# The query stage of a product-key expert layer in one pass or in two passes by tokens

## Chip, core and metric

The kernel runs on one core of one Trainium2 chip. The metric is the device time of one execution in microseconds (us); lower is better. TensorE does the matmuls, VectorE, ScalarE and POOL (GpSimd) the elementwise work, and SP issues most DMAs.

## What is computed

One step of a hybrid encoder layer for 512 prompt tokens and 128 sample tokens (640 in all, five tiles of 128). A recurrent group and a window attention feed `h = x + W_out [...]`; then a product-key expert layer is added, and this is the part that the change touches:

```python
def peer(xn, w_query, sub_keys1, sub_keys2, expert_u, expert_v):
    q = (xn @ w_query).reshape(T, PEER_HEADS, 2, D_HALF)          # 8 heads, two halves of 128
    s1 = jnp.einsum('thd,kd->thk', q[:, :, 0], sub_keys1)          # 128 keys each
    s2 = jnp.einsum('thd,kd->thk', q[:, :, 1], sub_keys2)
    v1, i1 = lax.top_k(s1, PEER_TOPK)                              # 16 best of each half
    v2, i2 = lax.top_k(s2, PEER_TOPK)
    cand_s = (v1[..., :, None] + v2[..., None, :]).reshape(T, PEER_HEADS, 256)
    ...
    top_s, top_pos = lax.top_k(cand_s, PEER_TOPK)
    idx = jnp.take_along_axis(cand_i, top_pos, axis=-1)            # of 16384 experts
    gates = jax.nn.softmax(top_s, axis=-1)
    u = expert_u[idx]
    act = jax.nn.gelu(jnp.einsum('thkd,td->thk', u, xn))
    return jnp.einsum('thk,thkd->td', gates * act, expert_v[idx])
```

## The kernel before

**Two ways to the experts.** The first 448 tokens (`SD`) go the dense way: all 16384 experts are multiplied with them, in `NS` = 64 pairs of 256 experts, first with the u slabs (lines 1285 to 1333), then with the v slabs (1339 to 1365); the gates stand as a matrix with zeros in DRAM (`Gd`). The last 64 prompt tokens and the 128 sample tokens are the "own" tokens (tiles 3 and 4): their expert rows are gathered by indirect DMAs on POOL's queue (`fetch`, line 1167), and VectorE multiplies or adds each row (`consume`, 1177). There are `NO` = 384 such rows of 128 x 1024, six buffers for them (`RING`), and `own_work` deals them out over the pairs once tile 4 is selected.

**Split operands.** Every slab of weights (128 x 2048, 1 MB) comes by an SP DMA into `raw` (`load_slab`, 88). ScalarE copies it into `wh` (`high`, 93), and VectorE or POOL subtracts to get the remainder `wl` (`low`, 98). Each of the three has two buffers. A product takes three matmuls for each of the eight blocks of the contraction: `wh` with `xh`, `wh` with `xl`, `wl` with `xh`. `next_slab` (222) prepares the next slab of the list `order` (213) and then issues the load of a later one.

**Query stage.** Each of the eight slabs of `w_query` holds 256 query columns of one head, hence two units of 128 columns: `u` from 0 to 15. Units 0 and 1 are computed in halves (`query_half`, 853) between the transposes of the five token tiles (`turn_rows`, 830), and the others in the loop from 939: `proj_T` (106) with 48 matmuls of 320 columns, then `query_keys(u - 2)` (907) with five score tiles, each an fp32 matmul that takes two instructions, two copies of the scores on ScalarE, and the search for the 16 best of each tile on VectorE; then, in every second unit, `next_slab(G)` with its subtraction on POOL; then the copy of the queries out of PSUM (`query_out`, 903). The schedule is manual: each engine runs its instructions in the order written.

**Plan of the pairs.** What is left of the selection is cut into pieces with estimated costs (`piece`, 988): for each tile `select` (candidates, `best` twice four times, `exponents` with an act on ScalarE, two `index`, `gates`), and for the dense tiles `matrix` (56 pieces `hot`, each with matmuls and copies). Lines 1201 to 1219 deal them out: tiles 4 and 3 first with at most 6.6 per pair, and the others evenly up to pair 58. In pair `c` VectorE runs the subtraction for slab `c + 1` (POOL does so for `c` up to 2), then `own_work(c)`, then the pieces of the pair.

Of the kernel before, what the change touches and what calls it, by code (L numbers as in the profile page):

```python
# [7 lines left out]
F32 = mybir.dt.float32  # L8
# [8 lines left out]
P = 128  # L17
# [4 lines left out]
T = S + NB * TS  # L22
# [26 lines left out]
def hybrid_layer(ctx: ExitStack, tc: tile.TileContext, i, o):  # L49
# [16 lines left out]
    def wide():  # L66
        return pss.tile([P, 2, 512], F32, name="pa", tag="pa", bufs=2)
# [35 lines left out]
    def kc(w, c=256):  # L103
        return [x.rearrange("p (k c) -> p k c", c=c) for x in w]
# [89 lines left out]
    for k in range(KD):  # L194
# [16 lines left out]


    order = [i["w_qkv"][0], i["w_u"][0], i["w_u"][1], i["w_qkv"][1], i["w_gate"][0], i["w_gate"][1]] \
        + [i["w_out"][n] for n in range(4)] + [i["w_query"][n] for n in range(PH)]
    slab_raw, slabs = [], []

    def fetch_slab():
# [604 lines left out]
    def mean_square(t):  # L822
        xn[t] = wk.tile([P, D], F32, name="xn", tag=("p", "pT")[t % 2], bufs=2)
        A.activation(xn[t], h_rows[:, t], AF.Square, accum_out=ssq[:, t:t + 1])
        rsqrt(rh, rv_h, ssq[:, t:t + 1], slice(t, t + 1), D)

    def scaled(t):
        V.scalar_tensor_tensor(xn[t], h_rows[:, t], rh[:, t:t + 1], g2b, op0=ALU.mult, op1=ALU.mult)

    def turn_rows(t, halves=(0, 1)):  # L830

        ts_ = slice(t * P, (t + 1) * P)
        for hf in halves:
            pt = bank().rearrange("p (k c) -> p k c", k=4)
            for k in range(4):
                PE.transpose(pt[:, k], xn[t][:, (4 * hf + k) * P:(4 * hf + k + 1) * P], ident)
            A.activation(xh[:, 4 * hf:4 * hf + 4, ts_], pt, AF.Copy)
            V.tensor_sub(xl[:, 4 * hf:4 * hf + 4, ts_], pt, xh[:, 4 * hf:4 * hf + 4, ts_].bitcast(F32))

    for t in range(NT):  # L840
        merge_attn(0, t)
    next_slab(V)
    for t in range(ND):
        merge_attn(1, t)
        nc.sync.dma_start(Hd[t], h_rows[:, t])
        if t:
            scaled(t - 1)
        mean_square(t)
    merge_attn(1, 4)
    xh, xl = parts_tile()  # L850
    two = [wide(), wide()]

    def query_half(n, hf):
        wh, wl = kc(slabs[A0 + 2])
# [5 lines left out]
    for hf in range(2):  # L860
        for t in range(3):
            turn_rows(t, (hf,))
    scaled(3)
    query_half(0, 0)
    mean_square(4)
    turn_rows(3)
    nc.sync.dma_start(X3, xn[3][HD:])
    scaled(4)
    nc.sync.dma_start(Xd, xn[ND])
    query_half(1, 0)  # L870
    turn_rows(4)
    for n in range(2):
        query_half(n, 1)
    close_wk()


# [23 lines left out]
    tq, close_tq = open_pool("tq")  # L900
    qt = {}

    def query_out(u, ps):
        q = qt[u] = tq.tile([P, T], F32, name="q", tag="q", bufs=2)
        A.activation(q.rearrange("p (a b) -> p a b", a=2), ps[:, :, :H2], AF.Copy)

    def query_keys(u):
        c, n = u // 2, u % 2
        s = tq.tile([P, NT, NK], F32, name="s", tag="s", bufs=2)
        q = qt.pop(u)  # L910
        for t0, t1 in ((0, 4), (4, 5)):
            sc = bank()[:, :(t1 - t0) * P]
            for t in range(t0, t1):
                PE.matmul(sc[:, (t - t0) * P:(t - t0 + 1) * P], q[:, t * P:(t + 1) * P], sk[n],  # L914
                          start=True, stop=True)
            A.activation(s[:, t0:t1].rearrange("p a b -> p (a b)"), sc, AF.Copy)
        for t in range(NT):
            v8, i8 = val[:, t, c, n], idx[:, t, c, n]
            V.max(v8[:, 0:8], s[:, t])
            V.max_index(i8[:, 0:8], v8[:, 0:8], s[:, t])  # L920
            s2 = tq.tile([P, NK], F32, name="s2", tag="s2", bufs=2)
            V.match_replace(s2, v8[:, 0:8], s[:, t], NEG)
            V.max(v8[:, 8:16], s2)
            V.max_index(i8[:, 8:16], v8[:, 8:16], s2)

    U = {}

# [4 lines left out]
        table[c][1] = high(table[c][0])  # L932
        table[c][2] = low(table[c][0], table[c][1], eng)

    Q0 = A0 + 2
    next_slab(G)
    query_out(0, two[0])
    query_out(1, two[1])
    for u in range(2, 2 * PH):
        c, n = u // 2, u % 2  # L940
        if n == 0 and c + 1 == PH:
            u_load(0)
        ps = wide()
        proj_T(ps, kc(slabs[Q0 + c]), xh, xl, n)
        query_keys(u - 2)
        if n == 0:
            if c + 1 < PH:
                next_slab(G)
            else:
                put(U, 0, G)  # L950
                u_load(1)
        query_out(u, ps)
    u_ps = {}

    def u_block(c, n):
# [7 lines left out]
    put(U, 1, G)  # L963
    query_keys(2 * PH - 2)
    u_block(0, 0)
    query_keys(2 * PH - 1)
# [10 lines left out]
    close_tq()  # L977

    Gd = dram.tile([NG, P, NCH, JG, TG], F32, name="Gd")
    Ad = [dram.tile([P, JG, SD], F32, name=f"Ad{n}", tag=f"Ad{n}") for n in range(NG)]  # L980
# [174 lines left out]
    matrix(ND - 1)  # L1155
    select(1)
    matrix(0)
    select(2)
    matrix(1)
    matrix(2)  # L1160


    NO = 2 * NR
# [37 lines left out]
    plan = [[] for _ in range(NS + 4)]  # L1201
    used, c = 0.0, 1
    for p in pieces[:n_own]:
        if used + p[0] > 6.6:
            used, c = 0.0, c + 1
        plan[c].append(p)
        used += p[0]
        if p[5]:
            used, c = 0.0, c + 1
    c0 = c  # L1210
    total = sum(p[0] for p in pieces[n_own:])
    used, c = 0.0, c + 1
    for p in pieces[n_own:]:
        while used >= total * (c - c0) / (NS - 6 - c0):
            c += 1
        plan[c].append(p)
        used += p[0]
        if p[5]:
            c += 1
    first = None  # L1220

    def own_work(c):

        nonlocal first
        if first is None:
            if "selected" in keep:
                first = c + 1
            return
        n0, n1 = [min(NO, NO * (x - first) // (2 * NS - 2 - first)) for x in (c, c + 1)]
        for n in sorted(rows):  # L1230
            consume(n)
            if n == NR - 1:
                own_acts()
        for n in range(n0, n1):
            fetch(n)

    Pv = {}

# [226 lines left out]
```

## Time and profile before

| | us |
|---|---|
| median of 3 runs | 1719.96 (1716.91 to 1726.47) |
| profiled execution, its own time | 1711.95 |
| span of the profiled execution | 1710.2 |
| TensorE busy in it | 1679.2 (98%) |
| VectorE busy | 1417.1 (83%) |
| ScalarE busy | 679.6 (40%) |
| POOL busy | 690.2 (40%) |
| query stage (units 0 to 15 on TensorE) | about 251 to 383 |
| u slabs | 383 to 1069 |
| v slabs | 1071 to 1703 |

Records are of one execution. PE is TensorE, PEld its weight loads, DVE VectorE, ACT ScalarE; L12 is line 12 of the kernel. Matmuls are pipelined, so the record of one is longer than the distance from one to the next, and it is the distance that counts. A wait is put down to the instruction whose semaphore came last.

### The profile page before, as it was taken

The page shows a single profiled execution, that of the slowest core. Times are in us where ns is not written, and L with a number is a line of the kernel's source. Part 1 is how long each engine was busy: PE and PEld are TensorE (multiplying, and loading weights), DVE is VectorE, ACT ScalarE, POOL GpSimd, SP SyncE. Part 2 cuts the span into 40 slices and gives each one's busy share as a digit, 9 for nine tenths or more (in the row PEclk, how much of TensorE's full clock was granted, in tenths as well). Part 3 has the DMA queues.
Part 4 walks back from the last instruction along what each step waited for, and adds up shares of the span by engine and source line. Part 5 has one row for each costly group of instructions (what it writes and reads, how often), then busy time and mean ns, then how long its engine had stood idle before and what let it go on. Part 6 is the DMA issues. An engine that isn't in the chain of part 4 may idle for free.

```text
span 1710.2 us, 24851 instructions
## 1 busy us (share of the span) xinstructions
PE 1679.2 (98%) x9654; PEld 1546.7 (90%) x9654; DVE 1417.1 (83%) x2348; ACT 679.6 (40%) x790; POOL 690.2 (40%) x485
## 2 busy tenths in 40 slices
PE   8999999999999999999999999899999999999998
PEld 8887889999989898999899999899998999999998
DVE  7766465999789999899988885788887888888886
ACT  5457332233444544554455553322232232232322
POOL 4122003233134344444444433455454555455551
PEclk9999899999999999999999999999999999999999
DMA  5313233223689898999999999999999999999995
GB/s 169 104 48 113 76 105 90 75 70 126 249 277 322 308 377 291 370 389 348 314 379 344 372 352 403 397 380 368 384 374 335 405 376 385 375 377 376 369 350 201
DMA packets 180983, 492.67 MB, mean 288 GB/s; under 512 B 16817, under 2 KB 75057, under 8 KB 170225
## 3 DMA queue, kind: packets, MB, share of 16 engines
q1 hardware_dynamic: 124848, 288.68, 46.7%
q0 software_dynamic: 55296, 201.35, 31.4%
q8 instruction: 75, 1.23, 0.3%
q10 hardware_dynamic: 720, 1.05, 0.2%
q14 instruction: 44, 0.35, 0.1%
HBM read 426.11 MB, written 65.48 MB: 287 GB/s over the span
## 4 chain that ended last, share of the span: by engine, by line
PE 75%; DVE 14%; DMA 5%; ACT 3%; issue 2%; POOL 0%; DVEq 0%; ACTq 0%; SPq 0%
PE po L1359 35%; PE pa L960 21%; PE pa L113 7%; PE pb L1134 3%; DVE wl L100 2%; DMA gt<-Gd 2%; PE pb L638 2%; PE pa L638 2%; DVE ring L1181 2%; DVE h_rows L1181 2%; DMA raw<-in_u 2%; PE pb L914 1%; PE pa L857 1%; ACT wh L95 1%; DMA Gd<-stage 1%
## 5 line engine op out<-in xcount | busy, mean ns | idle before, releaser
L1359 PE MATMUL po<-ph,wh 128*128 128x448 f32 x1024 | 374.7, 366 | 3.5 <-ACT act L1280 1.9
L1359 PE MATMUL po<-pl,wh 128*128 128x448 f32 x1024 | 374.9, 366 | 3.2 <-DVE pl L1273 3.2
L100 DVE TENSOR_TENSOR wl<-raw,wh 128x2048 fp32r<-128x2048 f32 x135 | 308.8, 2288 | 83.5 <-ACT wh L95 82.8
L960 PE MATMUL pa<-xh,wh 128*128 128x448 f32 x1024 | 377.5, 369 | 0.0
L1359 PE MATMUL po<-ph,wl 128*128 128x448 f32 x1024 | 374.5, 366 | 0.0
L960 PE MATMUL pa<-xh,wl 128*128 128x448 f32 x1024 | 374.2, 365 | 0.2 <-DVE wl L100 0.2
L960 PE MATMUL pa<-xl,wh 128*128 128x448 f32 x1024 | 374.1, 365 | 0.0
L95 ACT ACTIVATE wh<-raw 128x2048 fp32r<-128x2048 f32 x146 | 279.5, 1914 | 226.9 <-PE po L1359 173.8
L1174 POOL DMA_INDIRECT h_rows<-in_u_rows,rowi x96 | 138.5, 1443 | 219.9 <-DVE h_rows L1181 164.1
L1174 POOL DMA_INDIRECT ring<-in_u_rows,rowi x96 | 136.8, 1425 | 194.3 <-DVE ring L1181 173.4
L1174 POOL DMA_INDIRECT h_rows<-in_v,rowi x96 | 155.9, 1624 | 143.4 <-DVE h_rows L1186 121.3
L1359 PEld LDWEIGHTS po<-ph,wh 128*128 128x128 f32 x1024 | 192.7, 188 | 19.5 <-ACT act L1280 2.2
L1359 PEld LDWEIGHTS po<-pl,wh 128*128 128x128 f32 x1024 | 192.7, 188 | 19.0 <-DVE pl L1273 3.8
L960 PEld LDWEIGHTS pa<-xh,wl 128*128 128x128 f32 x1024 | 192.3, 188 | 16.1 <-DVE wl L100 0.6
L1359 PEld LDWEIGHTS po<-ph,wl 128*128 128x128 f32 x1024 | 192.7, 188 | 15.3
L960 PEld LDWEIGHTS pa<-xh,wh 128*128 128x128 f32 x1024 | 192.4, 188 | 15.2 <-ACT act L1280 0.3
L960 PEld LDWEIGHTS pa<-xl,wh 128*128 128x128 f32 x1024 | 192.5, 188 | 15.1
L1174 POOL DMA_INDIRECT ring<-in_v,rowi x96 | 149.8, 1560 | 133.2 <-DVE h_rows L1186 109.2
L1280 ACT ACTIVATE act<-pa 128x448 f32<-128x448 f32 x128 | 71.5, 559 | 232.4 <-PE pa L960 225.1
L1271 ACT ACTIVATE ph<-at 128x896 fp32r<-128x896 f32 x64 | 61.0, 953 | 254.0 <-DVE at L1266 254.0
L1142 ACT ACTIVATE stage<-pb 128x512 f32<-128x512 f32 x112 | 109.8, 1129 | 89.9 <-PE pb L1134 89.9
L1273 DVE TENSOR_TENSOR pl<-at,ph 128x896 fp32r<-128x896 f32 x64 | 69.9, 1093 | 72.7 <-ACT ph L1271 72.7
(280 smaller groups left out, 2498.7 us busy)
## 6 DMA issues: line engine op xcount, KB each, us to landing
raw<-in_u SPq DMA_DIRECT2D x64, 1024.0 KB
raw<-in_v SPq DMA_DIRECT2D x64, 1024.0 KB
Ad<-act SPq DMA_DIRECT2D x64, 448.0 KB
Gd<-stage SPq DMA_DIRECT2D x28, 1024.0 KB
gt<-Gd SPq DMA_DIRECT2D x64, 448.0 KB
at<-Ad SPq DMA_DIRECT2D x64, 448.0 KB
raw<-in_w_query SPq DMA_DIRECT2D x8, 1024.0 KB
raw<-in_w_out SPq DMA_DIRECT2D x4, 1024.0 KB
```

The source lines that it names most:

```text
L95: A.activation(wh, raw, AF.Copy)
L100: eng.tensor_sub(wl, raw, wh.bitcast(F32))
L113: PE.matmul(ps[:, hf, :H2], a[:, k, cs], b[:, k, hf * H2:(hf + 1) * H2], start=(k == 0 and n == 0), stop=(k == KD - 1 and n == 2))
L638: PE.matmul(ps, a[:, k0 + k, ts_], b[:, k, :], start=(k == 0 and n == 0), stop=(k == CT - 1 and n == 2))
L960: PE.matmul(u_ps[c, n][:, :SD], a[:, k, n * P:(n + 1) * P], b[:, k, :SD], start=(k == 0 and m == 0), stop=(k == KD - 1 and m == 2))
L1142: A.activation(d["stage"][:, :, t0:t0 + 4].rearrange("p j t -> p t j"), d[n, f], AF.Copy, scale=1.0 / GSC)
L1174: G.indirect_dma_start(out=rows[n], out_offset=None, in_=table, in_offset=bass.IndirectOffsetOnAxis(ap=rowi[:, c:c + 1], axis=0))
L1181: V.scalar_tensor_tensor(row, row, 1.0, xrow[:, n // NS_], op0=ALU.mult, op1=ALU.mult, accum_out=dots[:, n:n + 1])
L1271: A.activation(ph, a2, AF.Copy)
L1273: V.tensor_sub(pl, a2, ph.bitcast(F32))
L1280: A.activation(act[c][:, n], u_ps[c, n][:, :SD], AF.Gelu_apprx_tanh)
L1359: PE.matmul(po[k][:, :SD], a[:, j, k * P:(k + 1) * P], b[:, j, :], start=(c == 0 and j == 0 and n == 0), stop=(c == NS - 1 and j == 1 and ...
```

## The change

The query stage runs twice over the eight slabs: first for the 256 columns of tiles 3 and 4 (`OWN`), then for the 384 columns of tiles 0 to 2 (`DENSE`), so `order` holds the query slabs twice. The merges of the layer before are turned so that tiles 3 and 4 come first (`turns`). In the first loop the scores of a unit are searched at once. In the second loop VectorE gets the pieces of `select(ND)`, a budget of 4.2 of estimated cost per unit, then searches of the dense tiles; their scores wait in the three `stage` buffers (five units each) and one `act` buffer. After tile 4 is selected, each unit also fetches one own row and consumes the one before. The searches that are left become the first pieces of the pairs, all pieces are dealt out evenly over 58 pairs, and own rows start with pair 0. The queries and scores use the `act` buffers as scratch, and the pool `tq` is gone.

```diff
-        + [i["w_out"][n] for n in range(4)] + [i["w_query"][n] for n in range(PH)]
+        + [i["w_out"][n] for n in range(4)] + [i["w_query"][n] for _ in range(2) for n in range(PH)]
...
-    for t in range(NT):
+    turns = (ND - 1, ND) + tuple(range(ND - 1))
+    for t in turns:
         merge_attn(0, t)
     next_slab(V)
-    for t in range(ND):
+    for n, t in enumerate(turns):
         merge_attn(1, t)
-        nc.sync.dma_start(Hd[t], h_rows[:, t])
-        if t:
-            scaled(t - 1)
+        if t < ND:
+            nc.sync.dma_start(Hd[t], h_rows[:, t])
+        if n:
+            scaled(turns[n - 1])
+            if n == 1:
+                nc.sync.dma_start(X3, xn[ND - 1][HD:])
+            if n == 2:
+                nc.sync.dma_start(Xd, xn[ND])
         mean_square(t)
...
+    OWN, DENSE = slice((ND - 1) * P, T), slice(0, (ND - 1) * P)
+    def queries(ps, w, n, cols):
+        wh, wl = w
         for k in range(KD):
             for m, (a, b) in enumerate(((wh, xh), (wh, xl), (wl, xh))):
-                PE.matmul(two[n][:, hf, :H2], a[:, k, n * P:(n + 1) * P], b[:, k, hf * H2:(hf + 1) * H2],
+                PE.matmul(ps[:, :cols.stop - cols.start], a[:, k, n * P:(n + 1) * P], b[:, k, cols],
...
+    two = [wide()[:, 0], wide()[:, 0]]
+    turn_rows(ND - 1)
+    turn_rows(ND)
+    scaled(turns[-1])
     for n in range(2):
-        query_half(n, 1)
+        queries(two[n], kc(slabs[A0 + 2]), n, OWN)
+        turn_rows(n)
+    turn_rows(2)
...
+    def query_out(u, ps, cols):
+        x = qs[u] = scratch()
+        m = cols.stop - cols.start
+        A.activation(x[:, :m], ps[:, :m], AF.Copy)
+    def scores(u, m, s):
+        x = qs[u]
+        sc = bank()[:, :m * P]
+        for t in range(m):
+            PE.matmul(sc[:, t * P:(t + 1) * P], x[:, t * P:(t + 1) * P], sk[u % 2], start=True, stop=True)
+        A.activation(s, sc, AF.Copy)
...
-    for t in (ND, ND - 1):
-        select(t)
-    n_own = len(pieces)
-    select(0)
...
+    select(ND)
+    own_first = pieces[:]
+    del pieces[:]
...
+    def own_work(c):
+        own_step(*[n_pre + min(NO - n_pre, (NO - n_pre) * x // (2 * NS - 2)) for x in (c, c + 1)])
+    def own_keys(u):
+        s = qs[u][:, 2 * P:4 * P]
+        scores(u, 2, s)
+        search(u, own_tiles, s)
+    next_slab(G)
+    for u in range(2):
+        query_out(u, two[u], OWN)
+    for u in range(2, 2 * PH):
+        ps = wide()[:, 0]
+        queries(ps, kc(slabs[Q0 + u // 2]), u % 2, OWN)
+        own_keys(u - 2)
+        if u % 2 == 0:
+            next_slab(G)
+        query_out(u, ps, OWN)
+    todo, acts, sought, used = list(own_first), [], 0, 0.0
+    for u in range(2 * PH):
+        c, n = u // 2, u % 2
+        if n == 0 and c + 1 == PH:
+            u_load(0)
+        ps = wide()[:, 0]
+        queries(ps, kc(slabs[Q0 + PH + c]), n, DENSE)
+        if u < 2:
+            own_keys(2 * PH - 2 + u)
+        else:
+            scores(u - 2 + 2 * PH, 3, later(u - 2))
+        for f in acts:
+            f()
+        acts = []
+        if n == 0:
+            if c + 1 < PH:
+                next_slab(G)
+            else:
+                put(U, 0, G)
+                u_load(1)
+        query_out(u + 2 * PH, ps, DENSE)
+        if u < 1:
+            continue
+        used = max(used, 0.0) - 4.2
+        while used < 0:
+            if todo:
+                p = todo.pop(0)
+                p[2]()
+                used += p[0]
+                if p[4]:
+                    acts.append(p[4])
+                if p[5]:
+                    break
+            elif sought < u - 2:
+                search(sought, tiles, held_s[sought])
+                sought += 1
+                used += 5.0
+            else:
+                break
+        if not todo:
+            own_step(n_pre, n_pre + 1)
+            n_pre += 1
+    put(U, 1, G)
+    scores(4 * PH - 2, 3, later(2 * PH - 2))
+    u_block(0, 0)
+    scores(4 * PH - 1, 3, later(2 * PH - 1))
+    for u in (2 * PH - 1, *range(sought, 2 * PH - 1)):
+        piece(5.0, lambda u=u: search(u, tiles, held_s[u]))
+    rest_of_plan()
...
+    total = sum(p[0] for p in pieces)
+    used, c = 0.0, 0
+    for p in pieces:
+        while used >= total * (c + 1) / (NS - 6):
+            c += 1
+        plan[c].append(p)
```

## Rows read from the trace of the kernel before

**Rows 1.** Chain of waits in the query stage: start us, us, engine, tile, line.

```profile
276.25 7.04 PE pa L113 x48
283.30 1.11 PE pb L914 x10
```

**Rows 2.** TensorE's waits, 260 to 1090 us: waiter, releaser: total us, times, longest.

```profile
PE pb L1134 <- DVE ow L1126: 3.6, 4, 1.2
PE po L1359 <- DVE pl L1273: 2.6, 1, 2.6
PE po L1359 <- ACT act L1280: 1.9, 1, 1.9
```

**Rows 3.** Windows: length; busy us of PE, PEld, DVE, ACT, POOL; clock, DMA, GB/s.

```profile
300.00:320.00 20.00, 20.00 (x145) 20.00 (x144) 18.09 (x99) 5.89 (x10) 4.63 (x1) 1.00 0.31 104
424.00:1060.00 636.00, 631.33 (x3741) 580.79 (x3742) 565.68 (x936) 309.36 (x322) 261.48 (x183) 1.00 0.94 338
```

**Rows 4.** TensorE's timeline at line 186 (256 columns), then chain at line 638.

```profile
100.08 0.28 PE L186 MATMUL pb<-wl,xh 128*128 128x256 f32 x1
102.60 0.28 PE L186 MATMUL pb<-wl,xh 128*128 128x256 f32 x1
...
242.48 2.72 PE pb L638 x12
```

**Rows 5.** Timelines of ScalarE, then POOL: start us, us, instruction, idle before it.

```profile
276.07 0.77 ACT L916 ACTIVATE s<-pb 128x512 f32<-128x512 f32 x2 [7.23 <-PE pb L914]
276.72 1.92 ACT L95 ACTIVATE wh<-raw 128x2048 fp32r<-128x2048 f32 x1
...
278.71 4.63 POOL L100 TENSOR_TENSOR wl<-raw,wh 128x2048 fp32r<-128x2048 f32 x1 [11.53 <-ACT wh L95]
```

**Rows 6.** Window as a query slab's load ends, columns as in rows 3.

```profile
288.00:289.00 1.00, 1.00 (x9) 1.00 (x8) 0.93 (x7) 0.00 (x0) 0.00 (x0) 1.00 0.06 25
```

**Rows 7.** Chain of waits, then timelines of ScalarE and POOL, before the loop.

```profile
247.92 0.45 PE pb L836 x4
260.94 7.16 PE pa L857 x47
...
246.08 1.06 ACT L824 ACTIVATE xn<-h_rows 128x1024 f32<-128x1024 f32 x1 [1.52 <-DVE h_rows L652]
...
262.53 4.65 POOL L100 TENSOR_TENSOR wl<-raw,wh 128x2048 fp32r<-128x2048 f32 x1 [7.00 <-ACT wh L95]
```

**Rows 8.** Chain of waits at the act of `exponents` in a pair.

```profile
477.91 1.28 ACT L1045
479.52 1.80 ACT ix L1048
```

**Rows 9.** Line 1004 by durations (min/median/max); timelines of POOL and VectorE.

```profile
L1004 DVE TENSOR_TENSOR cand<-val x20: 209/284/4659, 406.4 to 762.2; 128x128 f32<-128x128 f32 x10, 128x192 f32<-128x192 f32 x5, 128x64 f32<-128x64 f32 x5
...
406.31 4.61 POOL L100 TENSOR_TENSOR wl<-raw,wh 128x2048 fp32r<-128x2048 f32 x1 [5.10 <-ACT wh L95]
...
276.70 0.29 DVE L919 MAX8 val<-s 128x8 f32<-128x128 f32 x1 [15.21 <-ACT s L916]
278.29 0.28 DVE L919 MAX8 val<-s 128x8 f32<-128x128 f32 x1
```

**Rows 10.** TensorE's timeline at the turn to v slabs; window there.

```profile
1069.04 0.37 PE L960 MATMUL pa<-xh,wl 128*128 128x448 f32 x1
1074.83 0.57 PE L1359 MATMUL po<-ph,wl 128*128 128x448 f32 x1
1075.20 0.57 PE L1359 MATMUL po<-ph,wh 128*128 128x448 f32 x1
...
1074.00:1075.00 1.00, 0.71 (x2) 0.67 (x3) 0.24 (x1) 1.00 (x1) 1.00 (x1) 0.50 0.85 313
```

**Rows 11.** Chain in the u stage, and a group of VectorE by line there.

```profile
423.94 53.38 PE pa L960 x262
...
L1181 DVE SCALAR_TENSOR_TENSOR h_rows<-h_rows,xrow 128x1024 f32<-128x1024 f32 x90 | 106.6, 1221 | 0.0
```

More of the change, by code (lines that the diff above doesn't have):

```diff
@@ L899, in hybrid_layer, with scratch, search @@
     idx = ta.tile([P, NT, PH, 2, TK], U32, name="idx")
[L900 to L907, printed above, removed]
-        c, n = u // 2, u % 2
[L909 to L917, printed above, removed]
+    qs = {}
+    def scratch():
+        return ap_.tile([P, 2, SD], F32, name="act", tag="act", bufs=3).rearrange("p a b -> p (a b)")
+    def search(u, tiles, s):
+        c, n = u // 2, u % 2
+        for m, t in enumerate(tiles):
+            st = s[:, m * NK:(m + 1) * NK]
             v8, i8 = val[:, t, c, n], idx[:, t, c, n]
[L919 to L922, printed above, removed]
+            V.max(v8[:, 0:8], st)
+            V.max_index(i8[:, 0:8], v8[:, 0:8], st)
+            s2 = tb.tile([P, NK], F32, name="s2", tag="s2")
+            V.match_replace(s2, v8[:, 0:8], st, NEG)
             V.max(v8[:, 8:16], s2)
             V.max_index(i8[:, 8:16], v8[:, 8:16], s2)
+    def query_out(u, ps, cols):
[8 more added lines that the diff above has]
+        A.activation(s, sc, AF.Copy)
     U = {}
@@ L933, in put @@
         table[c][2] = low(table[c][0], table[c][1], eng)
[L935 to L952, printed above, removed]
     u_ps = {}
@@ L961, in u_block @@
                           start=(k == 0 and m == 0), stop=(k == KD - 1 and m == 2))
[L963 to L966, printed above, removed]
     first_of = ta.tile([P, TK, TK], F16, name="first_of")
@@ L976, in hybrid_layer @@
     G.iota(io2, pattern=[[1, NK], [0, 2]], base=0, channel_multiplier=0, allow_small_or_imprecise_dtypes=True)
-    close_tq()
     Gd = dram.tile([NG, P, NCH, JG, TG], F32, name="Gd")
@@ L1149, in matrix, with later, rest_of_plan @@
             piece(2.4, lambda n=n: hot(n), pe=lambda n=n: place(n), act=lambda n=n: store(n))
-    for t in (ND, ND - 1):
-        select(t)
-    n_own = len(pieces)
-    select(0)
[L1155 to L1160, printed above, removed]
+    select(ND)
+    own_first = pieces[:]
+    del pieces[:]
+    held, held_s = [], {}
+    def later(u):
+        if u == 2 * PH - 1:
+            held_s[u] = qs[u + 2 * PH][:, 3 * P:6 * P]
+        else:
+            if u % 5 == 0:
+                held.append(tb.tile([P, NK, TG], F32, name="stage", tag="stage", bufs=3)
+                            .rearrange("p a b -> p (a b)"))
+            held_s[u] = held[u // 5][:, u % 5 * 3 * P:(u % 5 + 1) * 3 * P]
+        return held_s[u]
+    def rest_of_plan():
+        select(ND - 1)
+        select(0)
+        matrix(ND - 1)
+        select(1)
+        matrix(0)
+        select(2)
+        matrix(1)
+        matrix(2)
     NO = 2 * NR
@@ L1198, in hybrid_layer, with own_step @@
     NS = NK // 2
[L1201 to L1229, printed above, removed]
+    n_pre = 0
+    def own_step(n0, n1):
         for n in sorted(rows):
@@ L1235, in own_work @@
             fetch(n)
+    def own_work(c):
+        own_step(*[n_pre + min(NO - n_pre, (NO - n_pre) * x // (2 * NS - 2)) for x in (c, c + 1)])
+    Q0 = A0 + 2
+    own_tiles, tiles = (ND - 1, ND), tuple(range(ND - 1))
+    def own_keys(u):
[12 more added lines that the diff above has]
+        query_out(u, ps, OWN)
@@ new lines, in hybrid_layer @@
+    todo, acts, sought, used = list(own_first), [], 0, 0.0
[35 more added lines that the diff above has]
+                used += 5.0
+            else:
+                break
+        if not todo:
+            own_step(n_pre, n_pre + 1)
+            n_pre += 1
@@ new lines, in hybrid_layer @@
+    put(U, 1, G)
[5 more added lines that the diff above has]
+    rest_of_plan()
+    plan = [[] for _ in range(NS + 4)]
+    total = sum(p[0] for p in pieces)
[4 more added lines that the diff above has]
+        plan[c].append(p)
+        used += p[0]
+        if p[5]:
+            c += 1
```

16 lines of the change are left out of this document (removed).

## Prediction

> **What bounds the kernel now.** I read the busy times of the engines first, then the windows of the stages, then TensorE's waits, and then chain and timelines around the query stage. TensorE is busy for 98% of the span, but a busy record is not a full engine, so its spacing decides. In the query stage the chain shows one unit after the other without a gap: 48 projection matmuls of 320 columns in 7.04 us (146.5 ns each), then 10 score matmuls in 1.11 us, then the next unit [rows 1]: 8.15 us a unit. From 260 to 1090 us TensorE's waits sum to 10.0 us, of which 4.5 lie at the turn from u to v slabs and 3.6 are for `ow` [rows 2]. So TensorE sets the time nearly everywhere. VectorE is at 18.1 of 20 us in the query stage and at 566 of 636 us in most of the u stage [rows 3]. The change takes away no matmul column; by feeding TensorE better it can gain at most about 10 us.
>
> **Matmul work.** A unit of 24 weight blocks × two halves of 320 columns becomes 24 × 256 in the own pass and 24 × 384 in the dense pass. 256 columns come every 120 ns (21 steps in 2.52 us) and 512 every 227 ns (12 in 2.72 us) [rows 4]; between 320 and 512, 384 come out at 173 ns. 24 × (0.120 + 0.173) = 7.03 us: no difference. The five score tiles per unit (two instructions of 111 ns each) become two and three. A unit is then 24 × 0.120 + 4 × 0.111 = 3.33 us long in the own pass and 4.16 + 0.67 = 4.83 us in the dense pass.
>
> **Slabs, the step that decides.** Each query slab is now loaded and split twice: 8 more loads, 8 more copies `wh` on ScalarE of 1.92 us and 8 more subtractions `wl` on POOL of 4.63 us [rows 5]. What matters is their place. A slab's copy is issued in the first unit of the slab before it, on ScalarE behind that unit's copy of the scores, and this waits for the score matmuls, which TensorE runs behind the unit's projection. The rows show the order: scores end at 276.25, copy of the scores 276.07 to 276.72, `wh` from 276.72, POOL's `wl` 278.71 to 283.34 [rows 1, 5]. So the new slab is ready 7.09 us after the first unit's end, and TensorE, which needs `wl` at its third matmul, has only the second unit in between. Before, that is 8.15 us: 1.1 us to spare. After, it is 3.33 or 4.83 us. `wl` cannot hide, and all that TensorE has queued stands behind that third matmul.
>
> Own pass: 7.1 + 0.1 (the one score copy starts only when all scores are done) − 3.33 − 2 × 0.12 = 3.6 us a slab. Seven slabs are made in this loop (units 2, 4, ... 14): 25.4 us.
> Dense pass: a copy of 384 columns, 7.3 − 4.83 − 2 × 0.17 = 2.1 us; seven query slabs: 14.7 us. The first u slab is made the same way, with one more score block (0.33 us) ahead of its use: 1.8 us.
> Loads do not add: issued when `wl` has freed the raw buffer at 283.34, the next has moved by 289 [rows 6], so in under 6 us, and the use of that buffer is two slabs (over 20 us) later. TensorE's PSUM tiles do not add either: `query_out` stands behind `wh` on ScalarE, but its tile is wanted only two units later.
>
> **Front.** Now 247.92 to 268.1 us hold 14.06 us of projection, 4.5 us of transposes and 1.6 us of waits [rows 7]; query slab 2's `wl` runs from 262.53 to 267.18, and its `wh` before that, beside two projection halves (7 us) that hide both. After: tiles 3 and 4 are turned first, behind the `mean_square` of tile 2 on ScalarE (in the row 1.5 us behind the one before and 1.06 us long), so four copies and their remainders end near 253.0; 2.9 us projection, 0.9 transposes, 2.9 projection, 1.8 transposes end at 261.6, the last `xh` copy at 262.7, `wh` 264.6, `wl` 269.3. Nothing is left on TensorE to cover that: 7 us. Unit 2 starts effectively at 269.1, with 2 × 4.16 us of the dense halves still to do: 269.1 − 268.1 + 8.3 = 9.3 us.
>
> **Selection and own rows.** In the dense pass VectorE selects for tile 4 and begins the searches: by the planner's 4.2 per unit I count 9 searches done and 7 left for the first pairs, and 10 fetches ahead of the pairs. The act of `exponents` lands on ScalarE ahead of a `wh` (dense unit 4): table load 1.28, exponential 0.3 (to the next row), two copies of 1.80 [rows 8] = 5.2 us in the chain of that slab, on top of its 2.1.
> The extra `wl` also meet VectorE. In the trace the slowest add of candidates took 4.66 us where the median is 0.28; the first four began at 406.4, 0.1 us after a `wl` on POOL of 4.61 us [rows 9]; the searches beside `wl` keep 1.59 us a tile (276.70 to 278.29). The Trainium skill (SBUF — State Buffer, Who interferes with whom) says that a VectorE instruction with two SBUF inputs and a GpSimd one that reads SBUF exclude each other for a whole instruction; the trace agrees with its 4.66 us. The change puts own rows (1.22 us each, two SBUF inputs) [rows 11] beside seven such `wl`: VectorE can lose up to 4.6 us each time; POOL's `wl` can start up to 1.3 us late each time, 0 to 10 us in all. I take 3 us, near the lower end, since there is one own row per unit.
>
> **Clock.** Between the starts at 1069.04 and 1074.83 TensorE began two matmuls; the granted clock then was 0.50, the 1.2 GHz level, and matmuls of 448 columns came every 0.37 instead of 0.20 us [rows 10], 8 of them up to 1077.4: 1.4 us lost. The new waits are 2.1 to 7.3 us long, 15 of them. None (0 us) to all (15 × 1.4 = 21 us) may be followed by the lower level; the three waits nearest to that row (7.0, 7.3 and one of 3.6 us) I take as sure, of the rest one in ten: 6 us.
>
> **Later stages.** Per pair TensorE needs 48 × 0.2037 = 9.8 us [rows 11]; the 64 pairs take 383 to 1069 us, 10.7 each, so 0.9 go into placing and waits. VectorE: `wl` 2.3, own rows 376/126 = 2.98 × 1.30 = 3.9, pieces 4.5 (7 searches of 3 × 1.59, four selections of 23 by the planner's costs, 56 `hot` of 2.4, over 58 pairs) = 10.7 us. Now, in the same way: 2.3, 3.25 × 1.30 = 4.2 and 206/48 = 4.3, 10.8. So the pairs stay as tightly filled; a backlog from the dense pass can cost up to 15 us, fewer waits for `ow` give back up to 4. I take 3 us. The v stage waits for nothing after its start, and stays.
>
> **Sum.** 9.3 + 25.4 + 14.7 + 1.8 + 5.2 = 56.4 us from the chain of slabs; 3 port, 6 clock, 3 later stages: 68 us. 1711.95 (the profiled execution's time) + 68 = 1780; the median of the runs shown stands 1.0047 above the profiled execution: 1788 us.
>
> **Rivals.**
> 1. *The deep case:* TensorE falls to the lower level after nearly every wait (21 us instead of 6), the port costs its 10 instead of 3, and VectorE brings a backlog of 10 us into the pairs. For it: the 0.50 in the row, and VectorE's dense units at 4.7 + 1.3 us of work plus blocked time against 5.9 us of TensorE. Against: the row has nearly 5 us without work ahead of the lower level, more than 13 of the 15 waits. 1712 + 56 + 21 + 10 + 8 = 1807, as a median 1816.
> 2. *The shallow case:* part of the chain is hidden after all (the `exponents` act falls into a longer wait, front waits are shorter) and the earlier own rows relieve the pairs by up to 8 us: 1712 + 40 − 8 = 1744, as a median 1752.
> 3. *The other side, not slower:* the copy of the next slab does not wait for the first unit's scores, but starts when the slab before last is done. Then `wh` + `wl` + hand-overs, 6.7 us, stand against two units of 6.67 us and no slab is late; the front's 9 us stand against at most 10 us of regained waits: 1712, as a median 1720. It decides when the copy starts at least 3.3 us earlier. Against it: ScalarE takes its work in the order written, as its rows show.
> 4. *The change does not spread the searches,* as VectorE is full: they sit ahead of the first pairs, 7 × 4.7 = 33 us, of which `wl` ahead of need hides about 8: 1780 + 25, as a median 1813; no row of now separates it from rival 1.
>
> **How the numbers follow.** Forecast (1765 to 1805) 0.60; deep case and full VectorE together 0.20; shallow 0.12; other side 0.08, half of it within 0.5% and half faster. About 0.5%, 9 us, is what a measurement of this kernel tells from no change. The range 1755 to 1818 holds the forecast, half of the shallow and most of the deep case, some 0.83. Slower 0.92, same 0.04, faster 0.04.
>
> **What would show it.** In the own pass `wh` follows the score copy at once, `wl` at once behind it, and TensorE waits for `wl` on POOL about 3.6 us in every second unit, near 10.4 us from slab to slab; in the dense pass about 2.1 us, near 11.8, and once about 7; 1.2 GHz in the windows behind the longest waits. The query stage grows by about 60 us and TensorE's share falls to about 95%. I am wrong if these waits are missing or under 1 us; then rival 3 holds. A growing wait for VectorE's `wl` in the first pairs would be rivals 1 and 4.

## The result and the profile after

The changed kernel takes 1785.14 us (median of 4 runs, 1783.58 to 1788.19) where the kernel before takes 1721.49 us beside it (4 runs, 1716.91 to 1726.47): a ratio of 1.0371 [1.0338, 1.0405]. The profiled execution took 1785.43 us, with a span of 1783.7 us.

Page of the kernel after: busy us of each engine (share of the span), and the granted clock of TensorE in 40 slices.

```profile
PE 1705.6 (96%) x9654; PEld 1568.5 (88%) x9654; DVE 1428.3 (80%) x2348; ACT 693.0 (39%) x812; POOL 734.2 (41%) x493
PEclk9999898988999999999999999999999999999999
```

TensorE is now busy for 96% of the span instead of 98%, and three of the slices between 267 and 446 us show a granted clock under 0.9. Where the time lies is read from three rows of TensorE's timeline: the first projection matmul, the first u matmul and the first v matmul.

| us | first projection | first u | first v | query stage | u stage | rest |
|---|---|---|---|---|---|---|
| before | 250.84 | 383.04 | 1071.27 | 132.2 | 688.2 | 638.9 |
| after | 254.28 | 458.34 | 1146.40 | 204.1 | 688.1 | 637.3 |

Of the 73.5 us by which the span grew, 3.4 lie ahead of the first projection, 71.9 in the query stage, none in the u stage, and 1.6 came back behind it. The query stage, then.

TensorE's waits of the kernel after, 244 to 462 us (waiter, releaser: total us, times, longest); before, the same view had waits of 0.3 us at most in this stage:

```profile
PE pa L863 <- POOL wl L100: 42.1, 15, 4.0
PE pa L863 <- ACT act L921: 4.6, 2, 2.9
PE pa L863 <- ACT xh L837: 3.3, 1, 3.3
PE pa L947 <- POOL wl L100: 1.1, 1, 1.1
```

Fifteen waits for a `wl` on POOL: one in front, seven in the own pass, seven in the dense pass. The chain of waits shows how they stand, first in the own pass (start us, us, what), where [rows 1] had matmuls behind matmuls:

```profile
309.69 2.90 PE pa L863 x22
312.59 0.46 PE pb L928 x4
313.35 1.92 ACT wh L95
315.34 4.54 POOL wl L100
319.92 2.89 PE pa L863 x22
...
326.17 3.91 POOL wl L100
330.13 0.98 PE pa L863 x6
```

From 309.69 through 319.92 to 330.13 is one slab each: 10.2 us. Behind the scores of the slab's first unit (312.59) come the copy `wh` (313.35) and the remainder `wl` (315.34), and the next slab's third matmul waits for that. The timelines of ScalarE and POOL there answer to [rows 5]:

```profile
313.07 0.38 ACT L929 ACTIVATE act<-pb 128x256 f32<-128x256 f32 x1 [6.24 <-PE pb L928]
313.35 1.91 ACT L95 ACTIVATE wh<-raw 128x2048 fp32r<-128x2048 f32 x1
...
315.34 4.53 POOL L100 TENSOR_TENSOR wl<-raw,wh 128x2048 fp32r<-128x2048 f32 x1 [5.70 <-ACT wh L95]
```

ScalarE had been idle for 6.24 us when it copied the scores; the slab's copy, which needed nothing of them, stood behind that. In the dense pass the same order gives, in the chain of waits:

```profile
350.57 4.11 PE pa L863 x22
...
406.52 5.67 PE pa L863 x22
...
412.85 4.21 PE pa L863 x24
417.09 2.74 POOL wl L100
```

The next slab starts at 419.88, so a slab takes 13.4 us. Here 22 matmuls of 384 columns take 5.67 us and the next 24 only 4.21; in the first dense slab (350.57) the same 22, also behind a wait, took 4.11. The windows show why (length; busy us of PE, PEld, DVE, ACT, POOL; granted clock, DMA share, GB/s): own slabs early and late, then the first dense slab and a later one.

```profile
285.00:298.00 13.00, 9.47 (x56) 9.27 (x56) 6.24 (x35) 3.12 (x5) 4.73 (x2) 0.76 0.24 81
309.70:320.00 10.30, 6.97 (x57) 6.77 (x57) 6.15 (x33) 3.12 (x5) 4.53 (x1) 1.00 0.28 103
350.50:362.00 11.50, 9.51 (x56) 9.19 (x56) 4.97 (x26) 3.33 (x5) 4.57 (x2) 1.00 0.26 93
406.50:419.90 13.40, 11.57 (x61) 11.25 (x61) 5.86 (x27) 3.55 (x5) 6.70 (x3) 0.87 0.42 158
```

The granted clock falls in all seven dense slabs behind the first, in the middle of the slab's first projection (0.50 from 408 to 410 us), and is back before the second; the wait ahead is about 2 us, and longer once, at the `exponents` act. In the own pass and at the turn to the dense pass, waits of 3.5 us left it at 1.00 from 309.7 to 362, but not in the slabs before.

### The profile page after: what moved, and what is told of

Its sections match the earlier page's. It is cut to its first block, busy times and chain, and to the rows that moved or that the text cites. A ratio compares the mean times of both kernels' runs of the same rounds, so it can differ in the third digit from the quotient of the medians.

```text
span 1783.7 us, 24912 instructions
## 1 busy us (share of the span) xinstructions
PE 1705.6 (96%) x9654; PEld 1568.5 (88%) x9654; DVE 1428.3 (80%) x2348; ACT 693.0 (39%) x812; POOL 734.2 (41%) x493
## 3 DMA queue, kind: packets, MB, share of 16 engines
q8 instruction: 75, 1.23, 0.3%
## 4 chain that ended last, share of the span: by engine, by line
PE 75%; DVE 14%; POOL 4%; issue 2%; ACT 2%; DMA 2%; DVEq 0%; ACTq 0%; POOLq 0%
PE po L1415 34%; PE pa L947 24%; PE pa L863 5%; POOL wl L100 3%; PE pb L1116 3%; DVE wl L100 2%; PE pa L113 2%; DVE ring L1178 2%; DVE h_rows L1178 2%; PE pb L638 1%; PE pa L638 1%; ACT wh L95 1%; PE pb L186 1%; PE pb L399 1%; DVE eq L1043 0%
## 5 line engine op out<-in xcount | busy, mean ns | idle before, releaser
L95 ACT ACTIVATE wh<-raw 128x2048 fp32r<-128x2048 f32 x154 | 294.6, 1913 | 249.4 <-PE po L1415 200.7
L1171 POOL DMA_INDIRECT ring<-in_v,rowi x96 | 160.5, 1672 | 160.6 <-DVE h_rows L1183 134.6
L1171 POOL DMA_INDIRECT h_rows<-in_v,rowi x96 | 162.7, 1695 | 152.3 <-DVE h_rows L1183 127.9
L1171 POOL DMA_INDIRECT h_rows<-in_u_rows,rowi x96 | 131.9, 1374 | 191.9 <-DVE h_rows L1178 172.2
L100 POOL TENSOR_TENSOR wl<-raw,wh 128x2048 fp32r<-128x2048 f32 x19 | 87.0, 4578 | 109.6 <-ACT wh L95 109.6
```

The source lines that it names most:

```text
L95: A.activation(wh, raw, AF.Copy)
L100: eng.tensor_sub(wl, raw, wh.bitcast(F32))
L1171: G.indirect_dma_start(out=rows[n], out_offset=None, in_=table, in_offset=bass.IndirectOffsetOnAxis(ap=rowi[:, c:c + 1], axis=0))
```

## The experiments

The theory: the place of the slab's copy in ScalarE's order makes the time; the rivals are the lower clock behind each wait, POOL's 4.6 us subtraction, VectorE with the added searches and own rows, and the port between VectorE and POOL. No run leaves out any part of the computation. The runs are judged by two lengths, read as in the table above: the query stage (first projection to first u matmul) and the u stage (to the first v matmul), since the v stage varies by itself, as the last three runs show.

| us | median | ratio to before | query stage | u stage |
|---|---|---|---|---|
| before | 1716 to 1723 | 1 | 132.2 | 688.2 |
| after | 1785.14 | 1.0371 | 204.1 | 688.1 |
| e1_order | 1756.61 | 1.0226 [1.0178, 1.0274] | 154.7 | 698.4 |
| e2_front | 1792.27 | 1.0443 [1.0393, 1.0494] | 200.1 | 688.3 |
| e3_warm | 1782.26 | 1.0377 [1.0334, 1.0421] | 190.7 | 695.5 |
| e4_vector | 1780.61 | 1.0369 [1.0329, 1.0410] | 190.2 | 692.6 |
| e5_mended | 1735.84 | 1.0108 [1.0070, 1.0145] | 146.0 | 697.4 |
| e6_no_rows | 1742.44 | 1.0132 [1.0092, 1.0172] | 146.0 | 689.2 |
| e7_dense_v | 1739.81 | 1.0125 [1.0077, 1.0173] | 149.0 | 698.4 |
| e8_best | 1732.47 | 1.0071 [1.0039, 1.0103] | 143.0 | 689.3 |

**e1_order: the copy ahead of the scores.** In both loops:

```diff
-        own_keys(u - 2)
         if u % 2 == 0:
             next_slab(G)
+        own_keys(u - 2)
...
```

> The changed kernel (1785 us) with one difference in both query loops: the preparation of the next slab (ScalarE's copy, POOL's subtraction) is issued ahead of the unit's scores instead of behind them, so that the copy starts when the slab before last is free. Theory (the chain of slabs): own pass, wait for wl falls from 3.5 us a slab to about 0.6, dense pass from 2.5 to 0, and with it the 1.2 GHz stretches behind these waits; the front stays as it is. About 55 us less: 1730 us (1720 to 1740). Rival (VectorE's moved searches and own rows, or the port that it shares with POOL, hold the stage): TensorE finds another wait in the place of wl, over 1765 us.

Measured: 1756.61 us, 27 us over what I expected. The query stage fell by 49.4 us, and TensorE's waits, 244 to 462 us, show that the slab waits are what went:

```profile
PE pa L863 <- ACT act L921: 8.2, 2, 5.3
PE pa L947 <- DVE wl L100: 7.3, 1, 7.3
PE pa L863 <- POOL wl L100: 4.8, 4, 3.8
```

42.1 us of waits for POOL became 4.8, with the same number of subtractions on POOL. ScalarE's timeline in the own pass:

```profile
303.48 1.92 ACT L95 ACTIVATE wh<-raw 128x2048 fp32r<-128x2048 f32 x1
```

The copy starts beside its slab's third matmul (303.46), where in the changed kernel it comes 3.7 us behind it (313.35 against 309.69). So the place in ScalarE's order is the cause of these waits; that was the theory. But 10 us of the gain were given back: the u stage grew from 688.1 to 698.4, with 7.3 us of it in one wait for VectorE's `wl` at its beginning. Of the rest of the miss, 6 us are gain that the query stage did not bring, and 13 lie behind the first v matmul (the last runs). What fills VectorE is for e6 and e7 to tell.

**e2_front: the first slab earlier.** Query slab 2 is split behind tile 4's transposes, not behind those of all tiles:

```diff
     turn_rows(ND)
+    next_slab(G)
     scaled(turns[-1])
...
-    next_slab(G)
     for u in range(2):
         query_out(u, two[u], OWN)
```

> The changed kernel with one difference: the first next_slab(G), for query slab 2, is issued behind the transposes of tile 4 instead of behind those of tile 2. Theory: the 6.7 us of waits at unit 2 go, and perhaps the 1.2 GHz that follows (up to 5 us in the first slabs of the own pass); the waits of the loops stay: 1776 us (1772 to 1780). Rival (the front is held by the DMA that reads the scaled rows, not by the slab): 1785 us.

Measured: 1792.27 us; the query stage only 4 us shorter. Chain of waits at that place:

```profile
267.55 5.69 DMA sk<-in_sk
273.51 1.20 PE pb L929 x4
274.71 3.91 PE pa L863 x24
```

The wait for query slab 2's `wl` went, and the scores' first operand took its place: `sk`, loaded on SP's queue behind the rows for `xrow`, lands at 273.24, and TensorE waits 3.9 us for it. The lower clock stayed too (3.91 us for 24 matmuls that take 2.88 at 1.00). A wait at this place is replaced by the next late input; my theory had looked at one of them only. That the run is no faster than the changed kernel at all lies behind the first v matmul, where this execution took 649.4 us against 637.3, and which the edit does not touch (the last runs).

**e3_warm: the clock by itself.** TensorE gets matmuls into a PSUM tile that nobody reads, 12 ahead of each own slab and 9 ahead of each dense slab, so that it is busy while it would wait:

```diff
+    def warm(m):
+        idle = bank()
+        for _ in range(m):
+            PE.matmul(idle, xh[:, 0, :P], xh[:, 0, :512], start=True, stop=True)
...
+        if u % 2 == 0:
+            warm(12)
...
+        if n == 0:
+            warm(9)
```

> The changed kernel with matmuls added whose result nobody reads: 12 of 512 columns (2.7 us) ahead of each slab's first unit in the own pass, 9 (2.0 us) in the dense pass, in the place of the waits. Theory: the waits end at the same time, but the granted clock stays at 1.00, so the first unit of each slab loses nothing: dense slabs 11.9 us instead of 13.4, own slabs 10.2 all through, in all 12 to 17 us less, 1770 us (1766 to 1776). Rival (the lower clock falls into time that TensorE would wait anyway): 1785 us or a few us more for the added matmuls.

Measured: the query stage is 13.4 us shorter, with work added and nothing taken away. Chain of waits in the dense pass, and the window that answers to the first one shown of after (columns as there):

```profile
393.77 2.08 PE pb L1218 x9
395.84 4.23 PE pa L863 x24
...
400.74 4.21 PE pa L863 x24
...
285.00:298.00 13.00, 12.38 (x93) 11.66 (x92) 8.31 (x45) 5.50 (x8) 5.11 (x2) 1.00 0.29 97
```

Both projections of this dense slab take 4.2 us, and the early own slabs run at 1.00 where after shows 0.76. The lower clock remains in two slabs: that of unit 2 (4.39 us for 22 matmuls, 2.90 at 1.00) and the one behind the `exponents` act (5.66 us, 4.11 at 1.00). So the lower clock is a cost of its own, beside the waits that precede it, and some 12.5 us of it could be taken back; the other 0.8 of the 13.4 lie in the first projection, ahead of which no such matmul stands. The slab period in the own pass stayed at 10.3 us, the chain of `wh` and `wl`. The median shows only 3 us of the 13: the u stage grew by 7.4 us, with 8.4 us of waits for VectorE's `wl`, and what follows it by 5.0.

**e4_vector: the remainder on the faster engine, in the same place,** in both loops:

```diff
-            next_slab(G)
+            next_slab(V)
...
-                put(U, 0, G)
+                put(U, 0, V)
```

> The changed kernel (1785 us) with the subtractions of both query loops on VectorE (2.29 us) instead of POOL (4.6 us), in the same place. Theory (length of the chain decides): where VectorE is free the chain shortens by 2.3 us a slab; in the own pass VectorE first does the search of the unit before (3.1 us), so the wait falls from 3.5 to about 2.5 us; in the dense pass from 2.5 to near 0 where VectorE has no work queued. First u matmul at 430 to 440 instead of 458 us, 1765 us (1755 to 1775). Rival (VectorE's queue is longer than POOL's chain): 1785 us or more, with TensorE waiting for VectorE's wl.

Measured: 1780.61 us, query stage 13.9 us shorter. Chain of waits in the own pass:

```profile
300.33 2.20 DVE wl L100
302.57 4.39 PE pa L863 x22
...
311.10 2.20 DVE wl L100
```

`wl` takes 2.20 us of the chain instead of 4.5, but the searches of the scores ahead stand before it on VectorE, and a slab still comes only every 10.7 us here, part of it lost to the lower clock (4.39 for the 22 matmuls that take 2.90). Fourteen slabs times the 2.3 us saved would be 32 us; 13.9 came. The place counts for more than the engine.

**e5_mended: all known steps at once.** Each slab is split one unit earlier (odd units, right behind the last use of the buffer it replaces), the first one as in e2, the first two u slabs likewise, and tile 2's normalised rows go to another buffer than tile 4's:

```diff
-tag=("p", "pT")[t % 2]
+tag=("p", "pT")[t % 2 or t == 2]
...
-        own_keys(u - 2)
-        if u % 2 == 0:
+        if u % 2 == 1:
             next_slab(G)
+        own_keys(u - 2)
...
+        if n == 1:
+            if c + 2 < PH:
+                next_slab(G)
+            elif c + 2 == PH:
+                put(U, 0, G)
+                u_load(1)
+            else:
+                put(U, 1, G)
```

> The changed kernel with three differences: each slab is prepared right behind the last projection of the slab whose buffers it takes (odd units), the slab of unit 2 behind the transposes of tile 4, and the scaled rows of tile 2 take the buffer of tile 3 instead of that of tile 4, which a DMA still reads. Theory: all waits for wl go, the front keeps about 4 us, the pairs keep the 3 to 4 us that they gained: 1724 us (1715 to 1734), no faster than before beyond what can be measured. Rival 1 (the early own rows and moved searches do relieve the pairs once the slabs are in time): under 1712 us. Rival 2 (VectorE is full in the dense pass): over 1740 us, with TensorE waiting for VectorE's wl in the first pairs.

Measured: 1735.84 us; the query stage is down to 146.0 us, 58 less than in the changed kernel, and no wait for a `wl` on POOL is left. The u stage takes 697.4 us, 9 more. TensorE's waits, 244 to 462 us:

```profile
PE pa L948 <- DVE wl L100: 7.3, 1, 7.3
PE pa L863 <- ACT act L922: 7.0, 2, 4.1
```

At the first u slabs TensorE waits for VectorE and for nothing else over 0.4 us. VectorE does own rows in the dense pass (line 1179), and its timeline shows them, one beside POOL's `wl`:

```profile
364.03 1.21 DVE L1179 SCALAR_TENSOR_TENSOR h_rows<-h_rows,xrow 128x1024 f32<-128x1024 f32 x1
369.88 3.25 DVE L1179 SCALAR_TENSOR_TENSOR h_rows<-h_rows,xrow 128x1024 f32<-128x1024 f32 x1
377.78 5.08 DVE L1179 SCALAR_TENSOR_TENSOR h_rows<-h_rows,xrow 128x1024 f32<-128x1024 f32 x1
...
377.19 4.58 POOL L100 TENSOR_TENSOR wl<-raw,wh 128x2048 fp32r<-128x2048 f32 x1 [1.99 <-ACT wh L95]
```

The row begun at 377.78 lasts until 382.86, 1.1 us past the end of POOL's `wl` at 381.77, about the 1.2 us that a row takes by itself. Two causes are possible for the 9 us: the own rows at all in the dense pass, or their blocking by POOL. The next two runs take away one each.

**e6_no_rows: e5 with all own rows left to the pairs.** The pairs then do the rows that the dense pass had done.

```diff
-        if not todo:
-            own_step(n_pre, n_pre + 1)
-            n_pre += 1
```

> The mended kernel (e5_mended, 1736 us, first u matmul at 396, u stage of 696 us) without own rows in the dense pass: all 384 are fetched and consumed in the pairs. Theory (own rows, one of two blocked behind POOL's subtraction at the shared port, put VectorE behind): VectorE reaches the first pairs in time, TensorE's wait of 7.3 us for its wl goes, the u stage takes 686 us and starts at 396 as before: 1727 us. Rival (the searches alone fill VectorE): the wait stays over 5 us and the time at 1736 us. The searches and their order are the same.

**e7_dense_v: e5 with VectorE's subtractions in the dense pass,** so that no `wl` of POOL stands beside an own row there:

```diff
-                next_slab(G)
+                next_slab(V)
...
-                put(U, 0, G)
+                put(U, 0, V)
...
-                put(U, 1, G)
+                put(U, 1, V)
```

> The mended kernel (e5_mended) with the subtractions of the dense pass on VectorE (2.29 us each, eight of them: 18 us more work for it) instead of POOL (4.6 us). Theory (port): VectorE lost more to blocked instructions (own rows of 5.0 instead of 1.2 us, six or seven of them, and one of the index steps) than it now spends, so it is in the pairs no later than in e5_mended: TensorE's first wait for wl 0 to 7 us, 1730 us. Rival (VectorE is short of time, the port is a side matter): its backlog grows by 15 us or more, the wait at the first pairs grows to over 15 us, or TensorE waits for wl in the dense pass: over 1745 us.

Measured: u stage 689.2 us without the rows, as before the change, and 698.4 with the rows but without POOL. TensorE's waits for VectorE's `wl` from 380 to 1150 us, first e6, then e7:

```profile
PE pa L948 <- DVE wl L100: 3.4, 3, 1.6
```

```profile
PE pa L948 <- DVE wl L100: 11.0, 4, 4.1
```

In e5 the sum was 11.2 us. So it is the own rows in the dense pass that make VectorE late at the first pairs and lengthen the u stage by 8 us. How much of it is their own time and how much their blocking is not shown: e7's rows in the dense pass all take 1.2 us again, but its eight subtractions cost VectorE 2.3 us each, 18 in all, and its u stage is as long as e5's. Both medians stand above what was expected, and above e5's by 6.6 and 4.0 us. The kernel before took 4.6 us more beside them than beside e5 (1721.07 against 1716.45), and the intervals of the ratios overlap. In the traces, e6's execution has the same query stage as e5's and a u stage 8.2 us shorter, but its first projection starts 3.9 us later (253.71 against 249.77) and what follows the first v matmul is 14.8 us longer. The edit explains neither; the last runs account for 12 of the 14.8.

**e8_best: e6 with two copies moved up.** The copies of the projections go ahead of `next_slab` in front, and ahead of the `exponents` act in the dense pass:

```diff
-    next_slab(G)
     for u in range(2):
         query_out(u, two[u], OWN)
+    next_slab(G)
...
+        query_out(u + 2 * PH, ps, DENSE)
         for f in acts:
             f()
         acts = []
-        query_out(u + 2 * PH, ps, DENSE)
```

> e6_no_rows and two changes of order: the queries of units 0 and 1 are copied out ahead of the preparation of query slab 3, and in the dense pass ScalarE copies the queries out ahead of the act of the exponents. Theory: the waits for PSUM tiles (2.9 and 4.1 us) shrink to under 1.5 us each, the first u matmul comes at 388 to 391 us, the u stage takes 686 us: 1720 us (1713 to 1726), within what can be told from before (1716 us). Rival (with slabs in time the two passes gain): under 1708 us.

Measured: 1732.47 us (9 runs), the best of the two-pass kernels, and still 0.7% [0.4%, 1.0%] behind the kernel before. Query stage 143.0, u stage 689.3. TensorE's waits, 230 to 480 us:

```profile
PE pb L929 <- DMA sk<-in_sk: 3.4, 1, 3.4
PE pa L863 <- ACT act L922: 2.6, 2, 1.4
```

3.4 and 2.6 us lie within the query stage, 2.9 more come from the lower clock behind the wait for `sk` (in the chain, 1.19 and 5.01 us for pieces that take 0.44 and 2.88 elsewhere): 8.9 of the 10.8 us by which the stage is longer than before. By this sum, which no run tests, with every wait mended the two passes would be about as long as the one, not shorter.

**e9_order_again, e10_before_again, e11_best_again: three kernels once more, unchanged,** to see whether the v stage's pace belongs to the kernel.

> The kernel of the first experiment (next slab issued ahead of the scores) unchanged, for a second trace. In its first trace the 448-column matmuls of the v stage stood 207.0 and 207.95 ns apart (911 and 2051 of them in one piece of the chain each), where the kernel before shows 204.2 and 202.8. If this spacing belongs to the kernel (its order of instructions or its addresses), both pieces come again at 207 to 208 ns. If it belongs to the execution, at least one of them comes at 203 to 204 ns and the span is 4 to 13 us shorter than the 1758 us of the first trace. Independent of that, the first u matmul should come again at 410 us within 1 us and the u stage last 697 us within 2 us.

> The kernel before, unchanged, for a second trace. If the spacing belongs to the kernel, the v stage shows 204 and 203 ns again; if it belongs to the execution, it may show 207 ns in one of its parts, with the v stage 4 to 13 us longer than 631 us. The first u matmul should come at 383 us and the u stage last 688 us in both cases.

> The mended order without own rows in the dense pass (the eighth experiment) unchanged, for a second trace. First trace: first u matmul at 393.5 us, u stage 689 us, then 208.6 and 204.1 ns spacing. If the spacing belongs to the kernel, 208 to 209 and 204 ns again; if to the execution, other values between 203 and 208. The first u matmul should come within 1 us of 393.5 and the u stage last 689 us within 2 us either way, so that the kernel is 10 to 12 us behind the kernel before up to the v stage, whatever the spacing does behind it.

Measured: 1757.34, 1725.39 and 1730.74 us. The query stages came again at 154.9, 132.2 and 141.3 us, the u stages at 698.4, 690.6 and 694.6. The chain of waits of the v stage (matmuls of 448 columns in one piece), the kernel before, then e10, the same kernel:

```profile
1074.29 225.01 PE po L1359 x1102
1321.75 377.02 PE po L1359 x1859
```

```profile
1079.22 226.03 PE po L1359 x1102
1327.71 384.45 PE po L1359 x1859
```

Then the first pieces of e1 and e9, one kernel too:

```profile
1108.08 188.59 PE po L1415 x911
```

```profile
1108.72 184.96 PE po L1415 x911
```

These are averages of 204.2 and 202.8 ns a matmul before, 205.1 and 206.8 in e10, 207.0 in e1 and 203.0 in e9. Part of them is the lower clock at the turn to the v slabs [rows 10]. Read from one start to the next over stretches of 25 us, the distance is 202.7 or 206.7 ns in every trace, but for stretches in which it changes: before 202.7 throughout, e10 first 202.7 and from about 1325 us 206.7, e1 206.7 throughout, e9 first 202.7 and from about 1318 us 206.7. So the pace does not belong to the kernel. Nor does the chip alone set it: on the chip of e1, e5 runs at 202.7 throughout, and on the chip of e4, which does so too, e6 runs at 206.7. At 4 ns times some 3000 matmuls it moves a run by up to 12 us, which is the size of what the stages don't explain in e1, e2 and e6, all three at 206.7 in the whole v stage. e11's u stage holds a wait of 7.8 us at the turn to the v slabs where e8 has 2.7; without the difference the two agree.

## Why the prediction was right

The forecast was 1788 us in a range of 1755 to 1818; measured 1785.14. The mechanism was the one named: `wh` behind the score copy, `wl` behind `wh`, TensorE waiting in every second unit. By its own steps:

- **Own pass.** 10.4 us from slab to slab forecast, 10.2 measured at the full clock; 25.4 us forecast for seven waits, 7 × (10.2 − 6.66) = 24.8 measured without the clock.
- **Dense pass.** Forecast 11.8 us a slab, measured 13.4. The wait is as sized: 13.4 − 2 × 4.88 for matmuls − 1.55 for the clock (5.67 − 4.11) leaves 2.1 us, forecast 2.1. The clock is what was missing.
- **Exponents.** Forecast 5.2 us; the slab takes 17.5 us against 13.4 of the others, so 4.1. The act came without a table load; POOL's `wl` took 4.92. Timelines of ScalarE, POOL and VectorE:

```profile
382.34 3.70 ACT L1030 ACTIVATE ix<-it 128x2048 f16<-128x2048 f16 x2
385.94 1.90 ACT L95 ACTIVATE wh<-raw 128x2048 fp32r<-128x2048 f32 x1
...
387.91 4.92 POOL L100 TENSOR_TENSOR wl<-raw,wh 128x2048 fp32r<-128x2048 f32 x1 [12.59 <-ACT wh L95]
...
388.58 5.34 DVE L1041 TENSOR_TENSOR eq<-eq,ix 128x2048 f16<-128x2048 f16 x1
```

- **First u slab.** Forecast 1.8 us, measured 1.1.
- **Front.** Query slab 2 was to be ready at 269.3; it was at 273.2, so the 9.3 us became 13.2. The step that failed is that tile 2's `mean_square` follows the one before it: it writes the buffer of `xn[4]`, which a DMA still reads. Chain of waits, then ScalarE's timeline:

```profile
246.01 5.51 DMA Xd<-xn
...
251.62 1.06 ACT L824 ACTIVATE xn<-h_rows 128x1024 f32<-128x1024 f32 x1 [3.08 <-DMA Xd<-xn]
```

  The DMA had been there before the change, but tile 4 was then the last of the five, and no `mean_square` took its buffer over. I had counted what the moved step issues on ScalarE and not who else reads what it writes. The wait is 3.1 us, and the first projection runs at the lower clock behind it (5.27 us for 23 matmuls, 2.75 at the later pace), 2.5 us more; 3.9 of these 5.6 us came through.
- **Clock.** Forecast 6 us, measured about 19: 2.5 in front, 1.8 in unit 2's slab, 4.0 in the two own slabs behind it, and 1.5 to 1.6 in each of the seven dense ones (10.8), each against the same piece at a granted clock of 1.00. This is the mis-sized term. I had taken the three waits nearest to the 5 us of [rows 10] as sure and one in ten of the rest. The dense waits, the shortest of all at about 2 us, cost most in sum, and always; waits of 3.5 us stayed without cost from 309.7 to 362. Length alone was the wrong measure. 19 us lie just under the term's upper bound, 21 us.
- **Port.** Forecast 3 us on the chain, measured none to speak of: POOL's `wl` starts at once behind `wh` in the rows shown. VectorE pays: `eq` 5.34 us at 388.58 beside `wl` (the median of that line is 1.23), own rows up to 3.31 where the median is 1.22. The Trainium skill (SBUF — State Buffer, Who interferes with whom) has a VectorE instruction with two SBUF inputs and a GpSimd one that reads SBUF exclude each other; the trace agrees with 5.34 and, in e5, 5.08 us.
- **Later stages.** Forecast 3 us, measured −1.8 (u stage 688.1 against 688.2, the rest 637.3 against 638.9). The searches were spread as the change says, and the pairs took them: rival 4 fell, with waits for VectorE's `wl` of 2.0 us in all behind the first u matmul. The runs suggest that the slow dense pass, which gave VectorE time, has a part in that: where the query stage is shorter and the own rows stay in it (e1, e3, e4, e5, e7), the u stage is 4.5 to 10.3 us longer.

The sum: 68 us forecast between the profiled executions, 73.5 measured. The chain of slabs came out at its 56.4 (71.9 + 3.4 − 19 = 56.3), the port 3 and the later stages 5 under theirs, the clock 13 over: errors of opposite sign, so that the forecast was nearer than its terms, by luck. That it ends 3 us above the measured median instead of 5 below comes from the factor of 1.0047: the profiled execution of after stands at its median.

The rivals: the deep case was half right, 19 of its 21 us of clock came, its port and backlog did not (its sum adds 8 us for a backlog that its text puts at 10). The shallow case and the other side fell with the waits of 42.1 us. e1 shows the other side's mechanism by experiment: with the copy ahead of the scores it starts 3.6 us earlier, its condition was 3.3, and the 42.1 us became 4.8. Its time, no slower than before, did not come: e1 is still 2.3% behind, with 22.5 us more in the query stage and 10 in the u stage.

What it could have brought: even with most waits mended (e8) the query stage is not shorter than before, since TensorE's work in it was already without gaps [rows 1] and the two passes need the same 7.0 us of matmuls a unit. Most of the change's cost is the issue order: the swap of e1 takes 49.4 of the 71.9 us from the query stage, and the mended places of e5 take 58.0. Whether the two passes cost anything once all waits are gone is open; the best run stands 0.7% behind.

## What to carry to other kernels

When a loop's unit is cut in two, every preparation that was hidden by "one unit ahead" loses half its cover: work out the new unit against the whole chain of the next operand (copy, remainder, hand-overs), and issue the copy ahead of anything on that engine which waits for the unit itself. A step moved to the front of a stage must be followed through its buffers too: who still reads what it writes. And where TensorE is the bound, each new wait is to be priced with the slower matmuls behind it, here about three quarters of the wait itself in the dense pass (1.55 on 2.1 us).

## What the runs showed of the hardware

- A wait of about 2 us in the dense pass was followed each time by a stretch at the 1.2 GHz level inside the next projection (granted clock 0.50), 0.32 us between matmuls of 384 columns instead of 0.175, at a cost of 1.5 to 1.6 us; waits of 3.5 us from 309.7 to 362 were not. Filling the waits with matmuls that nobody reads kept the clock at 1.00 in all but two slabs and gave back some 12.5 us of the query stage.
- Matmuls of 448 columns in the v stage stand at one of two paces for hundreds of them, 202.7 or 206.7 ns, and partly at the other in the next execution of the same kernel, at a granted clock of 1.00 (e1, 1110 to 1290 us, at 206.7 ns; before, 1077 to 1300, at 202.7) and with no waits between them. Up to 12 us of 1720 hang on it. What sets it is open.
